# A hybrid DiT backbone on one core: attention queries staged in pairs, turned queries in the unused half of their tile, one square instruction per head

## The chip, the cores and the metric

The kernel runs on one core of a Trainium2 chip. The metric is the device time of one launch in microseconds (us). Three runs of the kernel before gave a median of 2776.6 us (2774.38 to 2782.41).

The core's engines each take their instructions in a fixed order: PE multiplies matrices (PEld is its weight load, which runs beside it), ACT applies functions element by element, DVE combines tensors, POOL does odd jobs and SP issues DMAs. An instruction starts when those ahead of it on its engine have started or ended and when the semaphores it names are reached.

## The reference

A latent stream of 256 tokens (a grid of 4 rows by 64) and a context of 256 tokens, both 2048 wide, go through two layers. Layer 0 mixes tokens by gated-DeltaNet heads (8 of width 128) beside neighbourhood-attention heads (8 of width 128), layer 1 by a short convolution; each has a SwiGLU block of 5632. What matters here is the mixer of layer 0:

```python
def even_mixer(h, hc, w_in, conv_w, a_log, dt_bias, gdn_norm, rpb, w_out, want_ctx):
    pc = hc @ w_in[:, :sum(EVEN_SEGS[:n_seg_c])]            # context: ka va kb vb a b
    ka_c, va_c, kb_c, vb_c, a_c, b_c = segs_c[:6]
    conv_c = short_conv_silu([ka_c, va_c], conv_w)
    k_c = l2norm(heads(conv_c[0]))
    ...
    o_c, s_ctx_fin = gdn_bidirectional(to_bhtd(q_c), to_bhtd(k_c), to_bhtd(v_c), g_c, beta_c, (zeros, zeros))
    ka, va, kb, vb, a, b, qa, qb, za = split_segments(h @ w_in, EVEN_SEGS)
    ka, va, qa = short_conv_silu([ka, va, qa], conv_w)       # conv of 5 taps along the tokens, then silu
    k_l = axial_rope(l2norm(heads(ka)))
    q_l = axial_rope(l2norm(heads(qa))) * HEAD_DIM ** -0.5
    o_l, _ = gdn_bidirectional(to_bhtd(q_l), to_bhtd(k_l), to_bhtd(heads(va)), g_l, beta_l, s_ctx_fin)
    y_gdn = gdn_out_norm(o_l, za, gdn_norm)
    y_na = neighbourhood_attention(heads(qb), heads(kb), heads(vb), k_ctx_na, v_ctx_na, rpb)
    return jnp.concatenate([y_gdn, y_na], axis=-1) @ w_out
```

`l2norm` divides a head's vector by the root of its sum of squares. The gated delta rule works in chunks of 64 tokens and needs the inverse of a triangular matrix for each.

## The kernel before

**Matmuls.** All products are float32 made of three products of rounded parts: each weight tile comes by DMA (`raw`, line 231, 512 KB, 4 buffers), ACT rounds it to `whi` (L174), DVE makes the rest `wlo` (L245), and PE multiplies `whi` by the activations' upper part, `wlo` by it, and `whi` by the lower part. `fm_stream` (matmuls L320) makes features on the partitions, `tm_stream` tokens. Activations of the layer stand in `hA` (first 2 of 16 blocks) and `hB`; `hC` is reloaded later.

**Streams of layer 0, in order.** Keys KA of the gated-delta heads, the gates, queries QA (two streams of four heads, latent tokens only, so 256 wide), values VA (two), and then the attention heads' queries QB (two streams, 256 wide), keys KB and values VB (in turn), the gate ZA, the output projection. Then come layer 0's SwiGLU and layer 1.

**A gated-delta head behind its stream.** `head_evac` makes the evacuation of four heads. `f` copies a head out of PSUM into `hst` (by L169 on ACT or L171 on DVE), and at the fourth head defers a list of steps, one for every step of the next stream: `front` is the convolution of 5 taps (L631 on ACT, four L634 on DVE) and the silu (L636) in a tile `cv` (4 buffers); `back` transposes it to tokens (PE, L193), copies it to `hq` (L174) and, for keys and queries, takes the sums of squares (`hss`, L665). A key head has four tiles of 128 tokens, a query head two, so `back` has four or two squares. `done` follows the fourth `back`. For keys it normalises `hq` (`rstd` with a root at L218 and DVE steps to L222; L681 on ACT; the rotary part L687 to L692 on DVE) and stores it to DRAM as `kd` (L705). For queries it does the same, transposes the result back into a tile `qf`, which is a buffer of the `cv` tag, and stores that as `qTd` (L725). `hq` has the shape [128, 4 token tiles, 4 heads, 128] and 2 buffers (tag `xdT`); a query head set fills 2 of the 4 token tiles.

**The gated-delta chain.** `chunk_matrices` loads the keys by token (`ktok`, L865), turns them (L193 on PE), makes decays (L858, exponential L860) and products (L894, L897), sends the triangles through DRAM (`nd`, `dl`) and solves 32 x 32 blocks in 31 pairs of DVE steps (L938, L940); the solution goes out as `dz` (L947) and comes back as `xd` and `xdT` (L968; `xdT` has the same tag as `hq`). `inverses` combines blocks on PE (L994, L1001, L1007) and `scan` runs the recurrence (L1032 to L1065). It is done for the context first and the latents second.

**Attention queries, keys, values.** `stage` copies a block out of PSUM into a 128 x 512 tile `nst` (3 buffers, tag `nst`), multiplies queries by the scale on the way (L1155, ACT), and stores it (L1156).

**What sets the order.** The program is written as Python generators; `drive` runs a stream and takes one deferred step after each of its steps, `pump` mixes in steps of the modulation (L404 loads, L409 on DVE, L416 on PE), and `plan` calls the inverses at counted steps (P_INV). Behind that a scheduler orders each engine's instructions by a simulated timeline, so a change of one instruction's cost or buffer can move others. On SP, too, a store stands in one row with the weight loads and waits its turn.

Of the kernel before, what the change touches and what calls it, by code (L numbers as in the profile page):

```python
# [23 lines left out]
F32 = mybir.dt.float32  # L24
F32R = mybir.dt.float32r
AF = mybir.ActivationFunctionType
OP = mybir.AluOpType
AX = mybir.AxisListType
# [10 lines left out]
CV = 4  # L39
# [9 lines left out]
R_QB = 0.6  # L49
R_KB = 1.8  # L50
R_ZA = 1.5
R_WO = 2.0
NST = 3
# [10 lines left out]
C_KA, C_VA, C_KB, C_VB, C_AB, C_QA, C_QB, C_ZA = 0, 1024, 2048, 3072, 4096, 4128, 5152, 6176  # L64
# [46 lines left out]
def body(tc, x, c, ctx, c_ctx, ada_w, ada_b, norm_mix, norm_ffn, ffn_w_gate, ffn_w_up, ffn_w_down,  # L111
# [3 lines left out]
    PE, ACT, DVE, POOL, SP = nc.tensor, nc.scalar, nc.vector, nc.gpsimd, nc.sync  # L115
# [43 lines left out]
    def smt():  # L159
        small.append(small.pop(0))  # L160
        return small[0].tile([128, 512], F32, name="sm", tag="sm")
# [3 lines left out]
    def copy(dst, src):  # L165

        flip[0] ^= 1
        if flip[0]:
            ACT.activation(dst, src, AF.Copy)  # L169
        else:  # L170
            DVE.tensor_copy(dst, src)  # L171

    def acopy(dst, src):
        ACT.activation(dst, src, AF.Copy)  # L174
# [16 lines left out]
    def transpose(dst, src):  # L191
        n = src.shape[0]
        return PE.transpose(dst, src, ident[:n, :n])  # L193
# [54 lines left out]
    def w_steps(segs, ks, behind=None):  # L248

        W = sum(s[2] for s in segs)  # L250
        nk = 1024 // W
        for g in range(0, len(ks), nk):
            assert ks[g + nk - 1] == ks[g] + nk - 1
            hi, lo = split_w(load_w(segs, ks[g], nk), behind if g // nk in (2, 3) else None)
            for j in range(nk):
                yield ks[g] + j, hi[:, j * W:(j + 1) * W], lo[:, j * W:(j + 1) * W]
# [3 lines left out]
    def grouped(steps, n, head=1):  # L260


        keep = []
        for i, (k, s) in enumerate(steps):
            keep.append(s)
            if i < head - 1:
                yield i, []
            elif i < n - TAIL:
                yield i, keep[:]
                keep.clear()  # L270
            elif i == n - 1:
                yield i, keep
            else:
                yield i, []
# [33 lines left out]
    def fm_stream(segs, ks, ws, evac, bank=None):  # L308

        nf = sum(s[2] for s in segs) // 128  # L310
        ps = [None] * nf
        for i, group in grouped(((k, (k, hi, lo)) for k, hi, lo in w_steps(segs, ks)), len(ks)):
            for f in range(nf):
                if i == 0:
                    ps[f] = (bank or mmt)()
                for g, (k, hi, lo) in enumerate(group):
                    a, b = hi[:, f * 128:(f + 1) * 128], lo[:, f * 128:(f + 1) * 128]
                    for j, (wt, mv) in enumerate(((a, 0), (a, 1), (b, 0))):
                        o = ps[f][:, 0:len(ws) * 256].rearrange("p (w t) -> p w t", w=len(ws))
                        last_mm[0] = PE.matmul(o, wt, h_(slice(0, len(ws)), mv, k), start=i == 0 and g == 0 and j == 0,  # L320
                                               stop=i == len(ks) - 1 and g == len(group) - 1 and j == 2).ins
                if i == len(ks) - 1:
                    evac(f, ps[f])
            yield
# [56 lines left out]
    def ada_close():  # L381

        for _ in closing[0]:
            yield
# [80 lines left out]
    def defer(f, *args):  # L465

        later.append((f, args))
# [9 lines left out]
    def drive(stream, pump=None, n=1, every=1, counts=False):  # L477
        for i, _ in enumerate(stream):
            steps[0] += counts
            while counts and plan and plan[0][0] <= steps[0]:  # L480
                plan.pop(0)[1]()
            if later and i % every == every - 1:
                f, args = later.pop(0)
                f(*args)
            if pump:
                pump(n)
# [6 lines left out]
    def h_(w, s, k):  # L493
        return hA[:, w, s, k, :] if k < KH else hB[0][:, w, s, k - KH, :]
# [20 lines left out]
    p = smt()  # L515
# [20 lines left out]
    wv = ev_w_in[0]  # L536
    ks = list(range(KT))
# [74 lines left out]
    scale = HD ** -0.5  # L612
# [26 lines left out]
    def head_evac(n, q, c0, done, sums):  # L639

        st_ = {}

        def f(i_, p):
            st_[i_] = kvp.tile([128, 512], F32, name="hst", tag="hst", bufs=6)[:, 0:n * 128]
            copy(st_[i_], p[:, 0:n * 128])
            if i_ < 3:
                return
            out_t = gw.tile([128, 4, 4, 128], F32, name="hq", tag="xdT", bufs=XDT)
            ss = kvp.tile([128, 4, 4], F32, name="hss", tag="hss", bufs=2) if sums else None
            cvs = {}  # L650

            def front(i):
                cvs[i] = conv_silu(st_[i], n // 2, c0 + q * 4 + i)

            def back(i):
                pt = smt()
                for t in range(n):
                    ins = transpose(pt[:, t * 128:(t + 1) * 128], cvs[i][:, t * 128:(t + 1) * 128])
                    if not t:
                        tc.keep_in_program_order(ins)  # L660
                acopy(out_t[:, 0:n, i, :], pt[:, 0:n * 128].rearrange("p (t e) -> p t e", t=n))
                if sums:
                    sq = kvp.tile([128, 128], F32, name="sq", tag="sq", bufs=1)
                    for t in range(n):
                        ACT.activation(sq, out_t[:, t, i, :], AF.Square, accum_out=ss[:, t, i:i + 1])  # L665


            for g_, i in ((front, 0), (front, 1), (front, 2), (back, 0), (front, 3), (back, 1), (None, 0), (back, 2), (back, 3)):
                if g_:
                    defer(g_, i)  # L670
                else:
                    defer(lambda: None)
            defer(done, out_t, ss)
        return f
# [38 lines left out]
    def qa_evac(q):  # L713
        def done(qt, ss):
            rq = rstd(kvp, ss[:, 0:2], [128, 2, 4], 8, 1.0, "rq")
            DVE.tensor_scalar(rq, rq, scale, None, op0=OP.mult)
            normalise(qt, 2, rq)
            for g in range(2):
                qf = kvp.tile([128, 2, 256], F32, name="qf", tag="cv", bufs=CV)
                pt = smt()  # L720
                for i in range(2):
                    for t in range(2):
                        transpose(pt[:, i * 256 + t * 128:i * 256 + (t + 1) * 128], qt[:, t, g * 2 + i, :])
                copy(qf, pt.rearrange("p (i e) -> p i e", i=2))
                SP.dma_start(qTd[:, q * 4 + g * 2:q * 4 + g * 2 + 2, :], qf)  # L725
        return head_evac(2, q, 16, done, True)
# [23 lines left out]
    kvp = pool("kv", stack=kvs, side="right")  # L750
# [7 lines left out]
    pump = Pump([ada_mixer(adap, [(2, "row", None), (3, "sh", None), (4, "sc", g_ffn[0])])], 1, 1)  # L758
# [330 lines left out]
    nsp = pool("stage", stack=lgs, side="right")  # L1089
# [54 lines left out]
    kb_d = dram.tile([128, 8, 512], F32, name="kb_d")  # L1144
    vb_d = dram.tile([128, 4, 1024], F32, name="vb_d")
    qb_d = dram.tile([128, 8, 256], F32, name="qb_d")

    def stage(dst, n, by=None):

        def f(i, *p):  # L1150
            st_ = nsp.tile([128, 512], F32, name="nst", tag="nst", bufs=NST)[:, 0:n]
            if by is None:
                copy(st_, p[-1][:, 0:n])
            else:
                ACT.activation(st_, p[-1][:, 0:n], AF.Copy, scale=by)  # L1155
            SP.dma_start(dst(i), st_)  # L1156
        return f

    for q in range(2):
        drive(fm_stream([(wv, C_QB + q * 512, 512)], ks, [0], stage(lambda f: qb_d[:, q * 4 + f, :], 256, scale)), pump, R_QB, counts=True)  # L1160
    for q in range(2):
        drive(fm_stream([(wv, C_KB + q * 512, 512)], ks, [0, 1], stage(lambda f: kb_d[:, q * 4 + f, :], 512)), pump, R_KB, counts=True)
        drive(tm_stream([(wv, C_VB + q * 512, 512)], ks, lhsh, [0, 1, 2, 3],
                        stage(lambda t: vb_d[:, t, q * 512:(q + 1) * 512], 512)), pump, R_KB, counts=True)
    lga.close()
    yp = pool("y", stack=lgs, side="right")

# [77 lines left out]
    held = na_scores(0)  # L1245
    for h in range(8):
        ahead = na_scores(h + 1) if h < 7 else None
        na_values(h, held)
        held = ahead
# [185 lines left out]
    pump = Pump([ada_job(adp, 1, 2, "row"), ada_job(adp, 1, 4, "sc", gamma=g_ffn[1]), ada_close()], PO, 68)  # L1435
# [7 lines left out]
    for half in range(2):  # L1443
# [17 lines left out]
        for f in range(8):  # L1461
            k = half * 8 + f
            p = smt()
# [5 lines left out]
            cv = dp.tile([128, 256], F32, name="ocv", tag="ocv", bufs=2)  # L1469
# [58 lines left out]
```

## Time and profile before

| | |
|---|---|
| median of three runs | 2776.6 us |
| the profiled execution: time / span | 2776.85 / 2775.1 us |
| granted PE clock, mean | 0.989 |
| instructions | 37687 |
| read from HBM / written | 659.21 / 23.10 MB |
| HBM rate over the span | 246 GB/s |
| PE's largest waits in 160 to 440 us | 6.4 us (ACT cv L636), 6.3 us (ACT nst L1155), 3.0 us (DVE hst L171) |
| squares L665 with their accumulator reads | 48 and 48, from 174.3 to 301.6 us |

The profiled execution took 1.75 us more than its span, which is what lies around it. A share of busy time is a mean over stages with different limits: streams of weights, in which PE never stops, and stages between them in which the chain of the gated-delta heads or the softmax of the attention heads makes it wait. The stages meant in the prediction are stretches of the span in us, and a stage is read by the engine whose busy time fills it and by what PE waits for in it. The chain of waits that ended last reaches back to 713 us only, so the changed place, at 160 to 440 us, is read from windows, waits and the timeline.

### The profile page before, as it was taken

The page shows a single profiled execution, that of the slowest core. Times are in us where ns is not written, and L with a number is a line of the kernel's source. Part 1 is how long each engine was busy: PE and PEld are TensorE (multiplying, and loading weights), DVE is VectorE, ACT ScalarE, POOL GpSimd, SP SyncE. Part 2 cuts the span into 40 slices and gives each one's busy share as a digit, 9 for nine tenths or more (in the row PEclk, how much of TensorE's full clock was granted, in tenths as well). Part 3 has the DMA queues.
Part 4 walks back from the last instruction along what each step waited for, and adds up shares of the span by engine and source line. Part 5 has one row for each costly group of instructions (what it writes and reads, how often), then busy time and mean ns, then how long its engine had stood idle before and what let it go on. Part 6 is the DMA issues. An engine that isn't in the chain of part 4 may idle for free.

```text
span 2775.1 us, 37687 instructions
## 1 busy us (share of the span) xinstructions
PE 2673.2 (96%) x13775; PEld 2192.5 (79%) x13775; DVE 1928.2 (69%) x2653; ACT 1289.3 (46%) x1923; POOL 52.5 (2%) x84
## 2 busy tenths in 40 slices
PE   5999999999989999999999999999999999999998
PEld 2588787887878788888888878788878888888886
DVE  2376786795768888888686667898688644445665
ACT  3267633333554544444455655444454444445554
POOL 0000000101000000000000000000000000000000
PEclk9999999999999999999999999999999999999999
DMA  9954478799748699999785558998669766666553
GB/s 345 325 182 152 146 239 280 233 319 281 231 157 279 227 330 337 347 337 325 276 276 194 193 160 287 328 325 294 199 200 337 239 195 189 187 201 208 195 192 127
DMA packets 287029, 684.81 MB, mean 247 GB/s; under 512 B 57209, under 2 KB 100833, under 8 KB 285307
## 3 DMA queue, kind: packets, MB, share of 16 engines
q1 hardware_dynamic: 280564, 669.26, 71.8%
q10 hardware_dynamic: 4375, 9.48, 1.0%
q0 software_dynamic: 1904, 3.67, 0.4%
q8 instruction: 108, 1.77, 0.2%
q14 instruction: 78, 0.64, 0.1%
HBM read 659.21 MB, written 23.10 MB: 246 GB/s over the span
## 4 chain that ended last, share of the span: by engine, by line
PE 61%; DMA 5%; DVE 4%; issue 3%; ACT 1%; POOLq 0%; POOL 0%; DVEq 0%; SPq 0%; ACTq 0%
PE mm L293 17%; PE mm L296 17%; PE mm L294 17%; DMA araw<-in_ada_w_dram 4%; PE mm L302 2%; PE mm L303 2%; PE mm L304 2%; PE sm L193 1%; DVE acc L374 1%; DVE wlo L245 1%; DMA acc<-in_ada_b_dram 0%; DMA raw<-in_ffn_w_gate_dram 0%; PE sm L1227 0%; PE gd L1074 0%; DVE xc L1301 0%
## 5 line engine op out<-in xcount | busy, mean ns | idle before, releaser
L174 ACT ACTIVATE whi<-raw 128x1024 fp32r<-128x1024 f32 x800 | 843.0, 1060 | 879.5 <-PE mm L296 627.3
L245 DVE TENSOR_TENSOR wlo<-raw,whi 128x1024 fp32r<-128x1024 f32 x800 | 969.7, 1221 | 401.2 <-ACT whi L174 394.4
L294 PE MATMUL mm<-wlo,fhi 128*128 128x512 f32 x1232 | 467.2, 390 | 0.0
L293 PE MATMUL mm<-whi,fhi 128*128 128x512 f32 x1232 | 465.3, 394 | 0.0
L296 PE MATMUL mm<-whi,flo 128*128 128x512 f32 x1232 | 390.5, 390 | 0.1
L374 DVE SCALAR_TENSOR_TENSOR acc<-araw,cT,acc 128x1024 f32<-128x1024 f32 x224 | 287.2, 1282 | 135.8 <-DMA araw<-in_ada_w_dram 125.7
L320 PE MATMUL mm<-hB,whi 128*128 128x512 f32 (+1 forms) x1064 | 278.0, 352 | 1.7 <-DVE hB L580 1.1
L296 PEld LDWEIGHTS mm<-whi,flo 128*128 128x128 f32 x1232 | 230.9, 188 | 49.0 <-DVE flo L1312 0.6
L293 PEld LDWEIGHTS mm<-whi,fhi 128*128 128x128 f32 x1232 | 231.6, 188 | 46.9
L294 PEld LDWEIGHTS mm<-wlo,fhi 128*128 128x128 f32 x1232 | 231.3, 188 | 46.0
L294 PE MATMUL mm<-wlo,ahi 128*128 128x512 f32 x672 | 255.2, 389 | 0.0
L293 PE MATMUL mm<-whi,ahi 128*128 128x512 f32 x672 | 254.4, 390 | 0.0
L320 PEld LDWEIGHTS mm<-hB,whi 128*128 128x128 f32 x1064 | 184.2, 192 | 34.5 <-issue 4.4
L296 PE MATMUL mm<-whi,alo 128*128 128x512 f32 x672 | 207.3, 389 | 0.0
L320 PE MATMUL mm<-hB,wlo 128*128 128x512 f32 (+1 forms) x532 | 180.2, 352 | 0.5 <-DVE wlo L245 0.5
L177 ACT ACTIVATE ahi<-prodT 128x256 fp32r<-128x256 f32 x176 | 73.0, 417 | 188.9 <-PE mm L294 181.9
L409 DVE SCALAR_TENSOR_TENSOR acc<-araw,cT,acc 128x512 f32<-128x512 f32 x192 | 142.5, 746 | 19.7 <-DMA araw<-in_ada_w_dram 16.2
L296 PEld LDWEIGHTS mm<-whi,alo 128*128 128x128 f32 x672 | 126.1, 188 | 26.3
L293 PEld LDWEIGHTS mm<-whi,ahi 128*128 128x128 f32 x672 | 126.2, 188 | 26.0
L294 PEld LDWEIGHTS mm<-wlo,ahi 128*128 128x128 f32 x672 | 126.0, 188 | 26.0
L178 DVE TENSOR_TENSOR alo<-prodT,ahi 128x256 fp32r<-128x256 f32 x176 | 74.3, 424 | 72.8 <-PE mm L296 67.7
L294 PE MATMUL mm<-wlo,dhi 128*128 128x512 f32 x336 | 122.9, 392 | 0.0
(398 smaller groups left out, 3474.7 us busy)
## 6 DMA issues: line engine op xcount, KB each, us to landing
araw<-in_ada_w_dram SPq DMA_DIRECT2D x288, 512.0 KB
raw<-in_ffn_w_down_dram SPq DMA_DIRECT2D x176, 512.0 KB
raw<-in_ffn_w_gate_dram SPq DMA_DIRECT2D x160, 512.0 KB
raw<-in_ffn_w_up_dram SPq DMA_DIRECT2D x160, 512.0 KB
raw<-in_ev_w_in_dram SPq DMA_DIRECT2D x112, 512.0 KB
araw<-in_ada_w_dram SPq DMA_DIRECT2D x192, 256.0 KB
raw<-in_od_w_in_dram SPq DMA_DIRECT2D x96, 512.0 KB
raw<-in_ev_w_out_dram SPq DMA_DIRECT2D x32, 512.0 KB
```

The costliest lines, as they stand in the source:

```text
L174: ACT.activation(dst, src, AF.Copy)
L177: ACT.activation(hi, src, AF.Copy)
L178: (eng or DVE).tensor_tensor(lo, src, hi, op=OP.subtract)
L245: last_lo[0] = DVE.tensor_tensor(lo, raw, hi, op=OP.subtract).ins
L293: PE.matmul(ps[ti][n], a, hi[:, n * 512:(n + 1) * 512], start=first, stop=False)
L294: PE.matmul(ps[ti][n], a, lo[:, n * 512:(n + 1) * 512], start=False, stop=False)
L296: last_mm[0] = PE.matmul(ps[ti][n], b, hi[:, n * 512:(n + 1) * 512], start=False, stop=False).ins
L302: PE.matmul(ps[ti][n], lh(t), hi[:, c_], start=False, stop=False)
L303: PE.matmul(ps[ti][n], lh(t), lo[:, c_], start=False, stop=False)
L320: last_mm[0] = PE.matmul(o, wt, h_(slice(0, len(ws)), mv, k), start=i == 0 and g == 0 and j == 0, stop=i == len(ks) - 1 and g == len(group ...
L374: DVE.scalar_tensor_tensor(acc, raw, cT[:, k:k + 1], acc, op0=OP.mult, op1=OP.add)
L409: DVE.scalar_tensor_tensor(accs[n], raws.pop(i), cT[:, k:k + 1], accs[n], op0=OP.mult, op1=OP.add)
```

## The change

It has three parts.

1. In `back` the squares of a head are one ACT instruction over all its token tiles into a tile of [128, 4, 128] with 2 buffers, and a DVE `tensor_reduce` sums them per token into `hss`. 48 squares with accumulator become 16 squares without and 16 reduces.
2. In `qa_evac` the turned queries are written into token tiles 2 and 3 of their own `hq` tile, in place of a `cv` buffer. A transposed half needs a 128 x 512 place, which one token tile of `hq` is.
3. `stage_pairs` puts two query blocks of 256 in one `nst` tile and stores both with one DMA of 256 KB: four stores in place of eight of 128 KB. `stage` is left with the full-width case.

```diff
@@ -660,9 +660,9 @@
                 acopy(out_t[:, 0:n, i, :], pt[:, 0:n * 128].rearrange("p (t e) -> p t e", t=n))
                 if sums:
-                    sq = kvp.tile([128, 128], F32, name="sq", tag="sq", bufs=1)
-                    for t in range(n):
-                        ACT.activation(sq, out_t[:, t, i, :], AF.Square, accum_out=ss[:, t, i:i + 1])
+                    sq = kvp.tile([128, 4, 128], F32, name="sq", tag="sq", bufs=2)[:, 0:n]
+                    ACT.activation(sq, out_t[:, 0:n, i, :], AF.Square)
+                    DVE.tensor_reduce(ss[:, 0:n, i], sq, axis=AX.X, op=OP.add)
@@ -716,7 +716,7 @@
             for g in range(2):
-                qf = kvp.tile([128, 2, 256], F32, name="qf", tag="cv", bufs=CV)
+                qf = qt[:, 2 + g].rearrange("p h e -> p (h e)").rearrange("p (i e) -> p i e", i=2)
                 pt = smt()
@@ -1145,23 +1145,32 @@
-    def stage(dst, n, by=None):
+    def stage(dst):
...
+    def stage_pairs(dst):
+
+        held = []
+
+        def f(i, p):
+            if not held:
+                held.append(nsp.tile([128, 512], F32, name="nst", tag="nst", bufs=NST).rearrange("p (f t) -> p f t", f=2))
+            ACT.activation(held[0][:, i % 2, :], p[:, 0:256], AF.Copy, scale=scale)
+            if i % 2:
+                SP.dma_start(dst(i - 1), held.pop())
+        return f
+
     for q in range(2):
-        drive(fm_stream([(wv, C_QB + q * 512, 512)], ks, [0], stage(lambda f: qb_d[:, q * 4 + f, :], 256, scale)), pump, R_QB, counts=True)
+        drive(fm_stream([(wv, C_QB + q * 512, 512)], ks, [0], stage_pairs(lambda f: qb_d[:, q * 4 + f:q * 4 + f + 2, :])), pump, R_QB, counts=True)
```

The lines of the changed kernel behind the second part keep their numbers; those behind `stage` are 9 higher.

The order moves. The first place is SP's row of DMAs around the key stores `kd`, before (`-`) and after (`+`): `raw` are weight loads, `ktok` the reloads of the keys, `kTd` and `qTd` stores of turned keys and queries.

```order
-L231 DMA raw<-in_ev_w_in_dram 128x2x512 x7
+L231 DMA raw<-in_ev_w_in_dram 128x2x512 x11
 L705 DMA kd<-hq 512x1x512
-L231 DMA raw<-in_ev_w_in_dram 128x2x512 x2
+L231 DMA raw<-in_ev_w_in_dram 128x2x512
 L865 DMA ktok<-kd 128x2x512
 L231 DMA raw<-in_ev_w_in_dram 128x2x512 x2
 L865 DMA ktok<-kd 128x2x512
 L884 DMA kTd<-kT 128x1024
-L725 DMA qTd<-qf 128x512
-L231 DMA raw<-in_ev_w_in_dram 128x2x512
-L725 DMA qTd<-qf 128x512
+L725 DMA qTd<-hq 128x512 x2
```

The second key store stands behind eleven weight loads since the `kTd` store before it, where it stood behind seven; the reloads of keys that follow it keep their distance to within one load.

The second place is ACT around the scaling of the second key set (`hq<-hq,rkr`), before:

```order
L174 ACTIVATE whi<-raw 128x1024
L665 ACTIVATE sq,hss<-hq 128x128
L681 ACTIVATE hq<-hq,rkr 128x128 x16
L174 ACTIVATE whi<-raw 128x1024
L218 ACTIVATE rqs<-rqv 128x8
L169 ACTIVATE hst<-mm 128x256 x2
L174 ACTIVATE whi<-raw 128x1024
L681 ACTIVATE hq<-hq,rqr 128x128 x8
```

and now:

```order
L636 ACTIVATE cv<-cv 128x256
L169 ACTIVATE hst<-mm 128x256 x2
L174 ACTIVATE whi<-raw 128x1024
L631 ACTIVATE cv<-hst,evcT 128x256
L174 ACTIVATE hq<-sm 128x2x128
L664 ACTIVATE sq<-hq 128x256
L631 ACTIVATE cv<-hst,evcT 128x256 x3
L681 ACTIVATE hq<-hq,rkr 128x128 x16
L218 ACT_TABLE_LOAD
```

The evacuation of the second query stream (`hst<-mm 128x256`) and its first taps (L631) stood behind the sixteen scalings of the keys and now stand ahead of them.

The third place is PE at the second set of inverses (L994, for the latents), which begins, before, inside the last products of a VB stream (`mm` with `hB`; L416 belongs to the modulation):

```order
L293 MATMUL mm<-whi,hB 128x512
L294 MATMUL mm<-wlo,hB 128x512
L296 MATMUL mm<-whi,hB 128x512
L416 MATMUL sm<-cs,acc 128x1 x3
L994 MATMUL gd<-xd,n_4634 32x32
L416 MATMUL sm<-cs,acc 128x1
L994 MATMUL gd<-xd,n_4634 32x32 x31
L302 MATMUL mm<-whi,hB 128x512
```

and now:

```order
L294 MATMUL mm<-wlo,hA 128x512
L296 MATMUL mm<-whi,hA 128x512 x2
L293 MATMUL mm<-whi,hA 128x512
L294 MATMUL mm<-wlo,hA 128x512
L296 MATMUL mm<-whi,hA 128x512
L1060 MATMUL gd<-vd,ktok 128x128 x4
L994 MATMUL gd<-xd,n_4606 32x32 x32
L293 MATMUL mm<-whi,hC 128x512
```

It begins behind the last products with `hA` and directly ahead of the first with the reloaded `hC`, which belong to the stream after. The first set of inverses, for the context, also stands later among the products, by some 20 us of them at their durations in the trace, and behind about 820 us of the profile before PE's order is the same in both.

More of the change, by code (lines that the diff above doesn't have):

```diff
@@ L1146, in body @@
     qb_d = dram.tile([128, 8, 256], F32, name="qb_d")
-    def stage(dst, n, by=None):
+    def stage(dst):
         def f(i, *p):
[L1151 to L1155, printed above, removed]
+            st_ = nsp.tile([128, 512], F32, name="nst", tag="nst", bufs=NST)
+            copy(st_, p[-1])
             SP.dma_start(dst(i), st_)
         return f
+    def stage_pairs(dst):
[7 more added lines that the diff above has]
+        return f
     for q in range(2):
-        drive(fm_stream([(wv, C_QB + q * 512, 512)], ks, [0], stage(lambda f: qb_d[:, q * 4 + f, :], 256, scale)), pump, R_QB, counts=True)
+        drive(fm_stream([(wv, C_QB + q * 512, 512)], ks, [0], stage_pairs(lambda f: qb_d[:, q * 4 + f:q * 4 + f + 2, :])), pump, R_QB, counts=True)
     for q in range(2):
-        drive(fm_stream([(wv, C_KB + q * 512, 512)], ks, [0, 1], stage(lambda f: kb_d[:, q * 4 + f, :], 512)), pump, R_KB, counts=True)
+        drive(fm_stream([(wv, C_KB + q * 512, 512)], ks, [0, 1], stage(lambda f: kb_d[:, q * 4 + f, :])), pump, R_KB, counts=True)
         drive(tm_stream([(wv, C_VB + q * 512, 512)], ks, lhsh, [0, 1, 2, 3],
-                        stage(lambda t: vb_d[:, t, q * 512:(q + 1) * 512], 512)), pump, R_KB, counts=True)
+                        stage(lambda t: vb_d[:, t, q * 512:(q + 1) * 512])), pump, R_KB, counts=True)
     lga.close()
```

## The prediction

> **What bounds the kernel now.** I read the page first (its engine line and its 40 slices), then busy time by stage, then what the matmul engine waits for in the stages that hold the changed lines.
>
> ```profile
> PE 2673.2 (96%) x13775; PEld 2192.5 (79%) x13775; DVE 1928.2 (69%) x2653; ACT 1289.3 (46%) x1923; POOL 52.5 (2%) x84
> ...
> core 0: us, PE busy (x) PEld busy (x) DVE busy (x) ACT busy (x) POOL busy (x), PEclk, DMA share, GB/s
> ...
> 0.00:160.00 160.00, 126.92 (x681) 77.25 (x682) 52.98 (x127) 44.95 (x65) 1.74 (x7) 1.00 0.95 320
> ...
> 219.00:257.00 38.00, 31.07 (x244) 30.18 (x243) 25.57 (x62) 37.47 (x105) 3.26 (x8) 0.94 0.31 90
> 257.00:314.00 57.00, 55.29 (x266) 45.66 (x266) 37.97 (x95) 40.13 (x89) 4.85 (x9) 0.95 0.42 136
> 314.00:367.00 53.00, 50.06 (x234) 41.58 (x235) 44.77 (x87) 22.41 (x31) 2.92 (x3) 0.97 0.61 187
> ...
> 391.00:420.00 29.00, 25.32 (x202) 24.43 (x202) 17.52 (x28) 8.19 (x11) 2.92 (x3) 1.00 0.87 277
> 420.00:440.00 20.00, 17.31 (x247) 13.19 (x247) 10.26 (x15) 6.07 (x12) 0.37 (x1) 0.91 0.88 261
> 440.00:640.00 200.00, 200.00 (x1342) 170.47 (x1341) 169.46 (x322) 63.95 (x116) 14.83 (x27) 1.00 0.84 282
> 640.00:680.00 40.00, 33.96 (x419) 26.35 (x418) 16.26 (x23) 10.78 (x17) 6.59 (x9) 0.83 0.94 260
> ```
>
> PE is busy 96% of the span, so the time falls only where PE has a hole. In 219–257 us it has one of 7 us, and there ACT is busy 37.47 of 38 us: that stage is bound by ACT, an engine with 46% of the span. All the changed lines run in 160–440 us. Behind it, 440–640 us has no hole at all, and its transfers run at 282 GB/s where the first 160 us reached 320, so a stream that starts earlier is fed earlier: what is won ahead of 440 us is carried on, unless 640–680 us takes it.
>
> PE's waits in 160–440 us (in all, times, longest), then their rows on PE's timeline (start, length, in brackets the idle time and who ended it), then the granted clock (behind the busy time) in short stretches:
>
> ```profile
> PE sm L193 <- ACT cv L636: 6.4, 3, 2.8
> PE mm L320 <- ACT nst L1155: 6.3, 4, 2.4
> PE mm L320 <- DVE hst L171: 3.0, 1, 3.0
> ```
> ```profile
> 233.06 0.44 PE L193 MATMUL sm<-cs,cv 128*128 128x128 f32 x2 [0.85 <-ACT cv L636]
> 241.22 0.44 PE L193 MATMUL sm<-cs,cv 128*128 128x128 f32 x2 [2.69 <-ACT cv L636]
> 256.77 1.19 PE L320 MATMUL mm<-hA,whi 128*128 128x512 f32 x2 [3.02 <-DVE hst L171]
> 331.54 1.12 PE L193 MATMUL sm<-cs,cv 128*128 128x128 f32 x4 [2.85 <-ACT cv L636]
> 399.71 0.51 PE L320 MATMUL mm<-hA,whi 128*128 128x256 f32 x2 [1.95 <-ACT nst L1155]
> 432.29 0.72 PE L320 MATMUL mm<-hA,whi 128*128 128x512 f32 x2 [2.45 <-ACT nst L1155]
> ```
> ```profile
> 242.20:245.50 3.30, 3.30 (x18) 0.50 0.32 76
> 255.70:262.60 6.90, 5.83 (x14) 0.51 0.50 175
> 330.85:334.20 3.35, 2.66 (x9) 0.50 0.40 142
> 433.20:436.60 3.40, 3.40 (x10) 0.51 1.04 379
> ```
>
> Three waits make up nearly all of the hole, each with a part of the change against it. And each idle of 2.45 us or more is followed by a stretch at half clock, which costs half of its busy time again: 1.65, 2.9, 1.35 and 1.7 us, together 7.6. The idles of 0.85 and 1.95 us are followed by none. The page "TensorE: Matmul & The Clock Gate" of the Trainium skill (Part 1: The HAM clock gate) puts the drop behind at least one idle window of about 3.4 us. The rows disagree about the length, not the halving.
>
> **The pairs** (stores of attention queries).
>
> ```profile
> ACT nst L1155 <- DMA qb_d<-nst: 15.6, 2, 7.8
> ACT cv L631 <- DMA qTd<-qf: 9.6, 3, 6.5
> ```
>
> ACT waited twice, 15.6 us in all, for a staging buffer whose store was not done, and PE behind it 1.95 and 2.45 us. Eight half-filled buffers become four full ones, with three to hold them: the first six feature blocks need no buffer back, where before only three did. Gain 1.95 + 2.45 + 1.7 of clock = **6.1 us**. Lower bound 2.0: the four KB blocks behind it use the same buffers, and the wait at 432.29 with its clock (4.1) could be handed to one of them. I take 6.1. Its evacuations stay eight, so nothing is added; one DMA of 256 KB replaces two of 128, and SP issues four fewer.
>
> **The queries' tile.** The second row above: ACT's conv tap waited 6.51 us at 328.82 for a `cv` buffer held by a turned-query store; a table load and the silu then run before PE's transposes at 331.54. Without `qf` in that pool the buffer is free. Gain 2.85 + 1.35 = **4.2 us**. The order keeps these stores behind weight loads, so that their tile, one of two, could be given back late to a VA head in the same way: lower bound 0. I take 4.2, and charge half of the 2.85, **1.4**, for a new wait of the silus, since their evacuations now stand in another order.
>
> **The squares.**
>
> ```profile
> L665 ACT ACTIVATE sq<-hq 128x128 f32<-128x128 f32 x48 | 14.6, 304 | 0.7
> L636 ACT ACTIVATE cv<-cv 128x512 f32<-128x512 f32 x16 | 9.7, 621 | 3.7 <-DVE cv L634 3.7
> L636 ACT ACTIVATE cv<-cv 128x256 f32<-128x256 f32 x8 | 3.2, 413 | 0.1
> L636 ACT ACT_TABLE_LOAD x8 | 10.3, 1283 | 0.1
> ```
> ```profile
> 174.28 0.30 ACT L665 ACTIVATE sq<-hq 128x128 f32<-128x128 f32 x1
> ...
> 174.70 0.31 ACT L665 ACTIVATE sq<-hq 128x128 f32<-128x128 f32 x1
> ```
> ```profile
> L1208 DVE TENSOR_REDUCE m<-sm x14: 678/682/692, 680.4 to 807.4; 128x1 f32<-128x512 f32 x14
> ```
>
> A square with its accumulator read takes a place of 0.42 us on ACT (174.28 to 174.70). Eight key heads have four, eight query heads two: 8 × 1.68 + 8 × 0.84 = 20.2 us. One instruction over the whole head is not in the trace; the silus of the same shapes take 0.62 and 0.41 us, so 8 × 0.62 + 8 × 0.41 = 8.2, and ACT gives up **12 us**. In the ACT-bound stage and around it that lifts the idles at 233.06, 241.22 and 256.77 (the hst copy there is late since ACT's and DVE's evacuations take turns): 0.85 + 2.69 + 3.02 + 1.65 + 2.9 = **11.1 us** on PE. Upper bound for more: ACT's 12 us. Lower bound 0, if DVE then holds the same evacuations.
>
> DVE gains 16 reduces. The nearest row reduces 512 elements in 0.68 us; half of that shape I put between 0.34 and 0.68: 8 × 0.68 + 8 × 0.41 = 8.7 us. They lie in stages where DVE is busy 25.57 of 38 and 37.97 of 57 us, so I take 0; without that cover the price is 8.7. The page "VectorE: DVE Perf Modes" of the Trainium skill says to expect the slowest pace of a `tensor_reduce` and to restructure where it is on the hot path, which speaks against this part. Its rule gives no price of its own here.
>
> ACT loads a table whenever its function changes between silu, exponential and root, 1.283 us a load. By the order of the instructions the region to 440 us loses three loads (cover for what is left, taken as 0) and the attention heads behind 680 us gain two in front of their exponentials: up to **2.6 us** back, at least 0 where PE has other work; I take it in full.
>
> **What is late next.** The gated-delta chain: key store, token-wise reload, chunk matrices, solve, inverse.
>
> ```profile
> 217.44 37.57 SPq L231 DMA_DIRECT2D raw<-in_ev_w_in_dram  x7
> ...
> 259.69 0.55 SPq L705 DMA_DIRECT2D kd<-hq  x1
> 260.79 1.73 SPq L231 DMA_DIRECT2D raw<-in_ev_w_in_dram  x2
> ...
> 268.74 4.50 SPq L231 DMA_DIRECT2D raw<-in_ev_w_in_dram  x2
> ```
> ```profile
> L994 PEld LDWEIGHTS gd<-xd,n x384: 101/108/154, 419.2 to 691.1; 32*32 32x32 f32 x128, 64*64 64x64 f32 x64
> ```
>
> SP issues in order, and the second key store is moved behind four more weight loads. The fourth load after 259.69 went out by 273.24, 13.5 us later; less the 11.1 us that PE is ahead by then, the chain is 2.4 us later on the clock. Its first inverse (419.2 us, where PE's weight queue had been held) stands later in PE's order by stream matmuls that take about 19.6 us at their durations in the trace, while PE comes 21.4 us earlier: 1.8 us early. PE would wait there 2.4 + 1.8 = **4.2 us**, between 0 (other steps of the chain have slack) and the 13.5 + 1.8 = 15.3 of no compensation.
>
> **Sum.** −6.1 − 4.2 − 11.1 + 1.4 + 2.6 + 4.2 = −13.2 us from the profiled run's 2776.85, whose span is 2775.1 with 1.75 around it; the median shown is 2776.6, the same for this purpose. Forecast **2764 us**. Moved alone to its worse end, the squares' gain (0) gives 2775, the reduces (8.7) 2772, the chain (15.3) 2775; the new costs all at nothing give 2764 − 4.2 − 2.6 − 1.4 = 2756.
>
> **Rivals.**
>
> *The chain sets the pace.* If the key store slips by the full 13.5 us, PE waits 15.3 at the inverse: −21.4 + 1.4 + 2.6 + 15.3 = −2.1, **2775 us** (2778 with 2.9 of half clock behind it). For it: the weight queue was already held there. Against: the solve's DVE steps lie between stream work, and order leaves 19.6 us more for them.
>
> *Slower, by the SP queue.* In the ACT-bound stage seven loads took 37.57 us, 5.4 each. If the four loads ahead of the key store go at that pace, the store slips 21.5 us, the inverse waits 23.3 and half clock follows it (2.9, as after 256.77), and the pairs keep only 2.0 of their 6.1 because their stores stand in the same queue: −21.4 + 4.1 + 1.4 + 2.6 + 23.3 + 2.9 = +12.9, **2790 us**. With the pairs at 2.0 the other terms come to −13.3, so it decides from 10.4 us of waiting at the first inverse with the clock's 2.9, and can be measured from some 19. Against it: behind 259.69 the loads went at 3.4 us each.
>
> *More is won.*
>
> ```profile
> 646.85 0.21 PE L994 MATMUL gd<-xd,n 32*32 32x32 f32 x2 [1.59 <-DMA xd<-dz]
> 669.54 0.77 PE L293 MATMUL mm<-whi,hC 128*128 128x512 f32 x1 [3.33 <-DMA hC<-h_d]
> ```
>
> 640–680 us has 6.0 us of idle and a clock of 0.83 (0.17 × 33.96 busy = 5.8 us). The second inverse now stands behind the value projection's last matmuls and no longer splits them, so these 11.8 us may go: **2752 us**. For: PE has other work there. Against: the solve that feeds it also stands later.
>
> *The half clock comes by itself.* The slow stretches could fall where they fall, with the 7.6 us staying: 2764 + 7.6 = **2771 us**. By the Trainium skill's window of 3.4 us, on the page named above, these idles would not be the cause. Each of the four stretches begins at such an idle, so I give it little.
>
> *The change frees nothing*: buffers are waited for as before by other tiles. **2777 us**. The order shows the evacuations at other places, which speaks against it.
>
> **How the numbers follow.** A run of this kernel can tell about 0.3% (8.3 us) from no change, so faster means under 2768.3 and slower over 2784.9. Forecast (2757 to 2768) 0.50; more won 0.11; chain 0.18; half clock by itself 0.05; nothing freed 0.05; slower by the queue 0.11. Faster is 0.50 + 0.11 = 0.61, the same 0.28, slower 0.11. The range takes in the chain with its clock, nothing freed, the single ends above and most of the larger gain's own spread: 2748 to 2780, leaving out 0.11 above and about 0.05 below.
>
> **What would show it.** Right: no PE idle over 1 us on nst L1155's successor, no DMA wait of `cv` on the turned queries, ACT clearly below full in the stage of 219–257, 16 squares and 16 reduces, clock 1.00 in those stages, and PE reaching the first hA matmuls of KB about 20 us earlier. The chain is told by a wait at the first L994 rows; the queue by the key store's time. Wrong would be: new half-clock stretches behind waits of silu or of `hq`, DVE full in 219–314 us, or a gain at 440 us that is gone at 680.

## The result and the profile after

The changed kernel took 2769.32 us in the median of ten runs (2762.71 to 2777.47), the kernel before 2776.72; the ratio is 0.9971 with a 95% interval of 0.9957 to 0.9985. One of the ten runs of the kernel before took 8001.77 us; the ratio leaves it out, and without it that median is 2776.6. By the ratio the change is some 8 us faster, surely more than nothing and just under the 0.3% that the prediction called measurable. Forecast were 2764, with a range of 2748 to 2780.

The page of the changed kernel, its engine line, and busy time by the same stages as in the prediction (engines in the same columns, then clock, DMA share and GB/s):

```profile
PE 2668.4 (96%) x13775; PEld 2192.5 (79%) x13775; DVE 1934.8 (70%) x2669; ACT 1280.7 (46%) x1842; POOL 53.7 (2%) x84
```
```profile
219.00:257.00 38.00, 36.12 (x269) 34.79 (x268) 34.02 (x80) 36.66 (x73) 2.78 (x8) 0.96 0.42 124
257.00:314.00 57.00, 57.00 (x289) 48.32 (x288) 41.88 (x97) 37.71 (x72) 4.15 (x9) 1.00 0.42 133
314.00:367.00 53.00, 53.00 (x320) 47.17 (x319) 50.16 (x97) 24.25 (x35) 2.93 (x3) 1.00 0.71 219
...
391.00:420.00 29.00, 29.00 (x164) 24.70 (x162) 17.06 (x22) 8.42 (x11) 1.43 (x2) 1.00 0.89 266
420.00:440.00 20.00, 19.29 (x283) 15.36 (x283) 15.26 (x23) 4.66 (x9) 0.52 (x1) 0.91 0.99 351
440.00:640.00 200.00, 193.33 (x1290) 164.79 (x1288) 160.24 (x310) 64.66 (x116) 20.82 (x33) 0.99 0.84 272
640.00:680.00 40.00, 31.94 (x565) 24.19 (x565) 21.57 (x37) 15.41 (x29) 2.53 (x2) 0.91 0.97 256
680.00:770.00 90.00, 84.53 (x468) 70.01 (x467) 61.46 (x116) 45.72 (x87) 0.00 (x0) 0.94 0.75 242
```

Ahead of 440 us the holes in the changed stages are nearly gone: PE is full in 257–314, 314–367 and 391–420 us and lacks 1.9 us in 219–257. Behind it there are new ones: 440–640 us had none before and has 6.7 us, 640–680 has 8.1 us where 6.0 were, 680–770 has 5.5 where 0.4 were. PE's waits ahead of 440 us and those of 600 to 770 us, after:

```profile
PE sm L193 <- ACT cv L636: 1.9, 1, 1.9
PE mm L320 <- ACT nst L1163: 1.4, 1, 1.4
PE gd L1007 <- issue: 0.7, 1, 0.7
```
```profile
PE gd L994 <- DMA xd<-dz: 9.4, 2, 5.9
PE gd L1052 <- DVE R L1035: 3.2, 1, 3.2
PE mm L293 <- ACT whi L174: 3.0, 2, 2.3
PE mm L293 <- DVE nst L171: 1.5, 1, 1.5
```

and the latter before:

```profile
PE mm L293 <- DMA hC<-h_d: 3.3, 1, 3.3
PE gd L994 <- DMA xd<-dz: 2.7, 3, 1.6
```

To weigh the two sides I cut the span at 440 us and at one instruction, the last product of the attention heads with their values (L1227, L1236 after), which every run but e2 (1.87 us) has with the same wait ahead of it. In before and after (window, its length, PE busy, clock):

```profile
0.00:440.00 440.00, 387.56 (x2441) 0.98 0.71 231
440.00:811.80 371.80, 356.45 (x2602) 0.98 0.78 254
```
```profile
0.00:440.00 440.00, 402.79 (x2569) 0.99 0.76 248
440.00:801.72 361.72, 333.68 (x2474) 0.97 0.77 241
```
```profile
811.80 3.49 PE L1227 MATMUL gd<-PT,vb 128*128 128x256 f32 x8 [3.67 <-ACT PT L169]
```
```profile
801.72 3.78 PE L1236 MATMUL gd<-PT,vb 128*128 128x256 f32 x8 [3.67 <-ACT PT L169]
```

PE's idle time up to 440 us fell from 52.4 to 37.2 us, by 15.2; from there to the mark it rose from 15.3 to 28.0, by 12.7. So only 2.5 us of the idle time won are left at the mark. PE's busy time up to it, for the same 5041 products, fell from 744.0 to 736.5 us, by 7.6. Together the mark comes 10.1 us earlier. What follows the mark is the same work in the same order; it took 1965.0 us of the profiled execution before and 1970.4 after, and between 1965 and 1976 in the other runs below, so a single execution does not show the lead exactly, and the ratio is what counts.

### The profile page after: what moved, and what is told of

It is laid out like the page before. It is cut to its first block, busy times and chain, and to the rows that moved or that the text cites. A ratio compares the mean times of both kernels' runs of the same rounds, so it can differ in the third digit from the quotient of the medians.

```text
span 2770.3 us, 37612 instructions
## 1 busy us (share of the span) xinstructions
PE 2668.4 (96%) x13775; PEld 2192.5 (79%) x13775; DVE 1934.8 (70%) x2669; ACT 1280.7 (46%) x1842; POOL 53.7 (2%) x84
## 5 line engine op out<-in xcount | busy, mean ns | idle before, releaser
L294 PEld LDWEIGHTS mm<-wlo,fhi 128*128 128x128 f32 x1232 | 231.8, 189 | 46.5 <-DVE wlo L245 0.3
```

The source lines that it names most:

```text
L294: PE.matmul(ps[ti][n], a, lo[:, n * 512:(n + 1) * 512], start=False, stop=False)
```

## The experiments

All run the kernel before on the same chip beside them; ratios are to that (over all runs, so they are not the quotients of the medians), and the times expected were set against 2776.7. Three theories came up: the chain (the data of the second inverses come no sooner), the order (the second inverses' new place costs), and, after the first four runs, SP's row (VB's stores behind the reloads).

**e1, the squares alone.**

```diff
-                        ACT.activation(sq, out_t[:, t, i, :], AF.Square, accum_out=ss[:, t, i:i + 1])
+                    ACT.activation(sq, out_t[:, 0:n, i, :], AF.Square)
+                    DVE.tensor_reduce(ss[:, 0:n, i], sq, axis=AX.X, op=OP.add)
```

> The squares alone (one ACT instruction a head, summed by DVE); tile and stores as before. The inverses keep their places of before in PE's order. Chain theory (what is won ahead of 440 us is cut down where PE meets the second set of inverses, whose data come no earlier than the solve and its round trip allow): PE's idles before L994 xd<-dz grow from 2.7 us in all to about 8, and the time is 2771 (between 2768 and 2774). Order theory (the loss comes from the second inverses' new place, right ahead of the first hC product): nothing is given back here, 2766 or less. Both: the idles of 0.85, 2.69 and 3.02 us behind ACT's evacuations go.

2768.1 us, ratio 0.9966 (0.9954 to 0.9978): the squares alone have the whole gain. The waits behind `cv` fell to 3.0 us and that behind `hst` is gone. Idle ahead of L994 was 4.0 us, not 8. Set against 2776.7 the ratio gives 2767.3 us, between the two theories, and the chain theory's sign did not come.

**e2, the tile alone.**

```diff
-                qf = kvp.tile([128, 2, 256], F32, name="qf", tag="cv", bufs=CV)
+                qf = qt[:, 2 + g].rearrange("p h e -> p (h e)").rearrange("p (i e) -> p i e", i=2)
```

> The queries' tile alone (turned queries leave from their own hq tile). Both theories: the 6.51 us that ACT waited for the turned-query store and PE's 2.85 us at 331 go, with the half clock behind them. Chain theory: 2775 (half of 4.2 kept). Order theory: 2773, all kept.

2780.03 us, ratio 1.0004 (0.9992 to 1.0015). The wait at 331 us went, but this order brings a new one ahead of 440 us, in PE's waits there:

```profile
PE mm L320 <- ACT whi L174: 7.4, 1, 7.4
PE mm L320 <- ACT nst L1155: 5.3, 3, 2.9
```

The stores of 128 KB are waited for as before; what keeps the rounding of weights back behind them was not followed up. Both theories had missed it.

**e3, the pairs alone** (the third part of the diff).

> The paired stores alone. The inverses now stand later in PE's order, the second nearly where the whole change has it. Both: PE's waits behind nst L1155 of 1.95 and 2.45 us go. Chain theory: 2773, since the gain ahead of 440 us (6) is smaller than what the chain can follow. Order theory: 2778 or more, because the new place of the second inverses costs more than the pairs win.

2776.32 us, ratio 0.9996 (0.9985 to 1.0007). The waits behind `nst` fell to 1.4 us, as expected, and the second inverses begin at the place of before in PE's order, to within three products, so the order theory did not apply; what came is another wait. PE's and DVE's largest from 600 us:

```profile
PE mm L293 <- DVE nst L171: 11.9, 1, 11.9
```
```profile
DVE nst L171 <- DMA vb_d<-nst: 13.7, 1, 13.7
```

DVE stands 13.7 us at a copy of the values VB, since its staging buffer's store has not gone out, and PE 11.9 us behind it.

**e4, squares and tile.**

> Squares and tile, stores of 128 KB as before; the inverses at their places of before. Chain theory: a bigger gain ahead of 440 us (15) meets the same chain: 2768 to 2771, little better than the squares alone, with some 10 us of idle before L994. Order theory: 2762, the whole of 15 kept.

2767.36 us, ratio 0.9959 (0.9946 to 0.9972): between the two theories, and no worse than the whole change, which has the pairs too. The DVE wait of the changed kernel for VB's store is the longest of its waits from 600 us:

```profile
DVE nst L171 <- DMA vb_d<-nst: 17.2, 1, 17.2
```

and SP's row shows the stores behind the reloads, in the changed kernel:

```profile
639.20 3.19 SPq L968 DMA_DIRECT2D xd<-dz  x2
642.49 0.43 SPq L865 DMA_DIRECT2D vtok<-vd__136  x1
643.02 1.44 SPq L1153 DMA_DIRECT2D vb_d<-nst  x3
```

The stores of three of VB's four blocks went out at 643.02, in one go. DVE had stood at the fourth copy since 634.3 and began it at 651.49. A DVE step that the inverses need (L1009) stands behind it in DVE's row; before, it stands ahead of the copy that waits. But the products whose results that step takes (L1007) ended at 650.78 only, so the copy held the step up by 1.4 us at most, and PE's own wait that names the copy is 1.5 us.

**e5, the whole change with VB's and KB's stores on POOL.**

```diff
-            SP.dma_start(dst(i), st_)
+            POOL.dma_start(dst(i), st_)
```

> The whole change, with the stores of attention keys and values (kb_d, vb_d) issued by POOL in place of SP. PE's order is the same up to the second inverses. SP-row theory (what the pairs win is lost because VB's stores stand in SP's row behind the reloads xd and xdT, so that DVE, at an nst copy, stands 17.2 us and holds back the scan's and the weights' DVE work): that wait falls under 5 us and the time to 2762 (2759 to 2765). Chain theory (the data of the second inverses come no sooner): PE still idles about 9 us before L994 xd<-dz and the time stays at 2767 to 2770.

2765.1 us, ratio 0.9951 (0.9934 to 0.9967); DVE's wait fell to 7.8 us (under 5 was expected), L994's from 9.4 to 4.7, idle behind 440 us from 28.0 to 21.0, and the mark came at 795.57. It is the lowest of all, though its interval meets that of the whole change.

The time is that of the SP-row theory, but the place is not. L994's wait is shorter mainly because PE came to it later: its block of 58 products began at 642.25 us, against 643.15 in the whole change. At the scan's product L1032 at 731 us PE is level with the whole change, and the lead of 6.2 us at the mark arises behind it. In the whole change:

```profile
730.60 1.16 PE L1032 MATMUL gd<-state,kT 128*128 128x128 f32 x8
736.29 2.08 PE L1052 MATMUL gd<-R,xdT 128*128 128x128 f32 x8 [3.20 <-DVE R L1035]
740.64 2.08 PE L293 MATMUL mm<-whi,yhi 128*128 128x512 f32 x4 [2.28 <-ACT whi L174]
748.29 1.06 PE L1032 MATMUL gd<-state,kT 128*128 128x128 f32 x8
```

and here, where PE has no wait between the same two:

```profile
730.86 1.06 PE L1032 MATMUL gd<-state,kT 128*128 128x128 f32 x8
744.53 1.06 PE L1032 MATMUL gd<-state,kT 128*128 128x128 f32 x8
```

Before, these two stand at 746.01 and 756.75 us with 0.3 us of idle between them. The whole change thus led by 15.4 us at the first of them and by 8.5 at the second. `R` is a DVE step of the scan; ahead of it in DVE's row stands the gate's `zst`, for which DVE waited 1.22 us while ACT loaded a table (from 732.58) and then made it. The other wait is for the first weights of the output projection. So neither theory is settled by this run: the data of the second inverses came hardly sooner, and what was won was won elsewhere.

**e6, the whole change with the xdT reloads on ACT.**

```diff
-                SP.dma_start(m_, dz[v, b, q].rearrange(...))
+                (ACT if v else SP).dma_start(m_, dz[v, b, q].rearrange(...))
```

> The whole change, with the xdT half of the reloads of the solve issued by ACT in place of SP. Chain theory: the eight xd loads no longer share a row with eight xdT loads and land some 4 to 6 us sooner, PE's idle before L994 falls from 9.4 to 4 us, and the time to 2764. SP-row theory: VB's stores go out some 5 us sooner, DVE's wait falls from 17 to about 12 us, 2766. If neither counts: 2769.

2773.38 us, ratio 0.9983 (0.9972 to 0.9994), slower than all three theories. The profiled execution took 2781.97 us, 8.6 more than the median, so its waits are larger than the run's usual ones. The reloads did land sooner: the wait for `xd` is gone from PE's list of 600 to 770 us, and DVE's for VB's store fell to 10.9 us. Others took their place:

```profile
PE mm L293 <- DVE nst L171: 8.7, 1, 8.7
PE gd L1052 <- DVE R L1035: 6.9, 1, 6.9
PE gd L994 <- ACT xdT L1011: 4.6, 1, 4.6
PE gd L994 <- issue: 3.4, 1, 3.4
```

**e7, squares and pairs.**

> Squares and pairs, the turned queries in a cv buffer as before. If the tile is worth its 4.2 us beside the others: 2773. If it is worth nothing (as alone): 2769, with the 17 us wait of DVE at VB's nst copy and some 9 us of idle before L994, as in the whole change.

2774.08 us, ratio 0.9987 (0.9976 to 0.9998), with DVE's wait of 15.3 us. Set against the whole change (0.9971) the tile is worth some 4 us beside the other two, though the two intervals meet; alone it was worth nothing.

**e8, squares and tile with VB's and KB's stores on POOL.**

> Squares and tile without the pairs, kb_d and vb_d stores issued by POOL. SP-row theory: DVE's wait at the nst copy of VB (5.2 us in the run of squares and tile) goes, 2763. Chain theory: 2767, as without it.

2767.83 us, ratio 0.9966 (0.9952 to 0.9979): DVE's wait at `nst` is gone, as expected, and nothing is won; PE now idles 7.2 us for `R` (L1035), 6.9 of it at the place where the whole change waits for it.

**e9, the pairs alone with VB's and KB's stores on POOL.**

> The pairs alone, with kb_d and vb_d stores issued by POOL; PE's order is that of the pairs alone up to the second inverses. SP-row theory: PE's 11.9 us behind DVE's nst copy of VB (pairs alone) falls under 4 us and the last L1236 row, at 807.6 there, comes 8 us sooner; 2768. If DVE's wait was only a sign of the chain behind it, PE idles as long elsewhere before 680 us and the time stays at 2776.

2777.86 us, ratio 1.0000 (0.9988 to 1.0013). The wait for DVE's copy is gone, and PE idles as long at the next load, the attention queries' `qb`, which is the second case that was expected:

```profile
PE sm L1212 <- DMA qb<-qb_d: 13.1, 1, 13.1
PE gd L1032 <- DVE state L1065: 5.1, 1, 5.1
```

**e10, the kernel before with VB's and KB's stores on POOL, the control.**

> The kernel before with kb_d and vb_d stores issued by POOL, a control: there DVE waited 2.5 us for a VB store and PE not at all, so SP-row theory gives 2775 (2773 to 2778). If the POOL row helps for another reason (fewer entries in SP's row in general), it gains as in the whole change: 2771 or less.

2785.58 us, ratio 1.0026 (1.0015 to 1.0038): neither case. Idle behind 440 us is 7.5 us more, and 7.2 us of waiting for `R` came at the place where the whole change has it too; the kernel before has 0.3 us of idle there.

**e11, the whole change with both rows moved** (e5 and e6 together).

> The whole change with kb_d and vb_d stores on POOL and the xdT reloads on ACT: both suspects of the second inverses at once. If each of the two rows is a bound of its own: no DVE wait over 4 us at nst, under 3 us of idle before L994, 2758 to 2762. If moving reloads to ACT holds up something else there (as the run with it alone was slower): 2765 or more.

2770.91 us, ratio 0.9971 (0.9960 to 0.9981), as the whole change. PE's wait for `xd` is gone and 9.4 us stand ahead of L994 for `xdT` on ACT, 5.3 for `qb`. Two suspects removed, the same time.

**e12, pairs and tile.**

> Pairs and tile without the squares. The squares carry the gain: 2774 to 2777, with the idles of 3.0 us behind hst and those behind cv at 230 to 260 us still there. If pairs and tile have a worth together that neither has alone: 2770 or less.

2770.53 us, ratio 0.9970 (0.9956 to 0.9984). The idles behind `cv` and `hst` are there (3.6 and 3.0 us), as expected for no squares, and still the kernel is as fast as with them. Two parts that are worth nothing alone are worth the whole gain together.

The whole table, from PE's busy time in the profiled execution of each. Idle is the window less that; "at `R`" is the part of it between the two L1032 rows shown with e5; the mark is the last product named above; tables are ACT's table loads from 680 to 830 us; VB is how SP's row has the second VB stream's four stores:

| parts | idle to 440 | 440 to mark | at `R` | mark | tables | VB stores | ratio |
|---|---|---|---|---|---|---|---|
| before | 52.4 | 15.3 | 0.3 | 811.80 | 7 | 1, 2, 1 | |
| squares | 45.0 | 18.0 | 0.3 | 802.66 | 7 | 1, 2, 1 | 0.9966 |
| tile | 54.8 | 16.5 | 0.0 | 809.08 | 5 | 1, 2, 1 | 1.0004 |
| pairs | 46.5 | 27.6 | 0.0 | 807.59 | 5 | 3, 1 | 0.9996 |
| squares, tile | 41.9 | 17.8 | 0.3 | 799.59 | 7 | 1, 2, 1 | 0.9959 |
| squares, pairs | 40.1 | 28.1 | 6.9 | 809.65 | 9 | 3, 1 | 0.9987 |
| pairs, tile | 44.6 | 17.5 | 0.3 | 800.74 | 7 | 1, 2, 1 | 0.9970 |
| all (after) | 37.2 | 28.0 | 5.5 | 801.72 | 9 | 3, 1 | 0.9971 |
| all, stores on POOL | 38.3 | 21.0 | 0.0 | 795.57 | 7 | (POOL) | 0.9951 |
| all, xdT on ACT | 39.3 | 33.6 | 6.9 | 812.00 | 9 | 3, 1 | 0.9983 |
| all, both | 37.9 | 27.7 | 0.0 | 800.60 | 5 | (POOL) | 0.9971 |
| squares, tile, stores on POOL | 44.2 | 23.0 | 6.9 | 802.73 | 9 | (POOL) | 0.9966 |
| pairs, stores on POOL | 46.9 | 27.6 | 0.0 | 811.78 | 7 | (POOL) | 1.0000 |
| before, stores on POOL | 51.4 | 22.9 | 7.2 | 814.13 | 9 | (POOL) | 1.0026 |

Each line is one execution; that of the pairs alone took 7.6 us more than its run's median, that of e6 8.6. Three things are seen. Up to 440 us every part counts: 7.4 us less idle for the squares, 5.9 for the pairs, 2 to 3 for the tile beside either or both (nothing alone), and 15.2 for all. Behind it, as long as the stores are on SP, the idle time is 15 to 18 us where the scheduler's order lets the first of VB's stores go out alone, and 28 to 34 where three go out in one go behind the reloads. Three of the four kernels with the pairs fell into the second order, pairs and tile into the first. With the stores on POOL the idle time is 21 to 28 us in all five, so VB's stores are not all of it. The third is the column "at `R`": five kernels idle 5.5 to 7.2 us there and all others 0.3 or less, and the five are those with nine table loads behind 680 us. In the same five SP issues seven loads of the output projection's weights in one row that takes 11.8 to 12.8 us. Which of these brings which was not tested.

## Why the prediction was right in direction and too large

*The pairs, 6.1 us; the tile, 4.2; the squares, 11.1.* Their places were right. The idles of 1.95 and 2.45, of 2.85, and of 0.85, 2.69 and 3.02 us are gone after, but for 1.88 us behind `cv` at 244 us, the kind of remainder for which 1.4 was charged, and 1.4 behind `nst`. Of the signs that the prediction named, the 16 squares and 16 reduces came, the wait of `cv` for the turned queries is gone, and KB's first products with `hA` start at 398.90 us, where they started at 420.24. Others did not come: ACT is still busy 36.66 of 38 us in 219–257, the clock there is 0.96, and half clock follows the silu's wait at 244 us, which was a sign of being wrong. As terms of the total they were wrong in kind: worth 9, 0 and 0 us alone in the order squares, tile, pairs, but none of them is worth a fixed sum beside the others.

*The prices of the new instructions.* Both were right. After, on ACT and DVE:

```profile
L664 ACT ACTIVATE sq<-hq 128x512 f32<-128x512 f32 x8 | 4.9, 629 | 0.0
L664 ACT ACTIVATE sq<-hq 128x256 f32<-128x256 f32 x8 | 3.1, 418 | 0.1
```
```profile
L665 DVE TENSOR_REDUCE hss<-sq 128x4 f32<-128x512 f32 x8 | 5.4, 680 | 0.1
L665 DVE TENSOR_REDUCE hss<-sq 128x2 f32<-128x256 f32 x8 | 3.2, 417 | 1.9 <-ACT sq L664 1.8
```

8.0 us on ACT against 8.2 forecast, 8.6 on DVE against 8.7, and no PE wait names the reduces. The prediction set the page "VectorE: DVE Perf Modes" of the Trainium skill (Rules for kernel authors) beside this part, which expects the slowest pace of a `tensor_reduce`. The 0.68 us above is that of a copy of the same size out of PSUM (L171, 683 ns in the trace), and moving the sums there paid: 0.9966 alone.

*The half clock, 7.6 us.* This term was too large. At half clock were 17.1 us up to 440 and 13.7 from there to the mark before, 6.8 and 21.3 after. An estimate of their price, half of PE's busy time in them, gives 7.7 and 6.2 us before, 3.4 and 6.3 after. So ahead of 440 us 4.3 of the 7.6 came: the stretches at 255.7 and 330.9 us went, and those at 242.2 and 433.2 have successors at 244.6 and 428.9. PE's busy time for the same products did fall by 7.6 us, but only 4.2 of it is the clock by this estimate; the rest was not traced, so the agreement is chance. Behind 440 us the new stretches lie in part where PE waits: in one of 10.2 us, 637 to 647, at L994, PE was busy 4.8 us. The rival "the half clock comes by itself" is right in that stretches still come, and wrong for those ahead of 440 us.

*The first inverses, 4.2 us.* This step failed. The key store did go out later in the row, but PE lost only 0.7 us at the first set. What the chain took back, it took at the second set, which the prediction had named only as a place to win: there I read the new place, behind VB's last products, as a gain. The second inverses' own wait grew from 2.7 to 9.4 us. PE reached them 12.1 us sooner than before (633.1 us against 645.3), while the `xd` reloads went out from 630.47 to 642.39, against 639.77 to 650.26, so 9.3 to 7.9 us sooner. With the scan and the weights behind it idle time grew by 12.7 us, where the sum had 4.2 for the chain and 2.6 for table loads.

*The table loads, 2.6 us.* They came as counted: three fewer up to 440 us (19 for 22), two more from 680 us on (9 for 7). Of PE's waits in 600 to 770 us only 0.5 us names the exponentials, but the place at `R`, where these loads stand, has 5.5 us of idle where it had 0.3. So the term may have been too small; that the loads are the cause there is argued from the table, not shown.

*The sum.* Idle: the terms had 13.8 less 1.4 won up to 440 us, and 15.2 came; they had 6.8 given back, and 12.7 came: 8.6 ahead of the L1032 at 731 us, 5.2 behind it at `R`, and 1.1 less in what follows. Clock: 7.6 were forecast, and PE's busy time fell by as much, 4.2 of it by the clock. That makes 10.1 at the mark against 13.2 forecast, and about 8 in the ratio. So the term most at fault is the payback: half of what it was, put at the wrong set of inverses, with the place at `R` counted only in part. That more idle time was won ahead of 440 us, and that the busy time fell beyond the clock, made up for some of it; that is luck.

*What is shown and what is not.* Shown: idle time up to 440 us falls with every part but the tile alone; how much of it is kept is decided behind 440 us, at the second inverses and at `R`; and in the order of the changed kernel VB's stores behind the reloads hold DVE (17.2 us). Not shown: that this wait is what costs the time. Taking the stores out of SP's row cuts the idle time behind 440 us by 7.0 in e5, but PE was level with the whole change until the place at `R`. With squares and tile (e8) the same step won nothing, with the pairs alone (e9) it only moved 12 us of waiting to another load, in the kernel before (e10) it cost 7.5 of idle, nearly all at `R`, and with both rows moved (e11) 9.4 us of waiting came for `xdT`. Open as well is what brings the wait at `R`: no kernel was made that changes only the table loads or only the weight loads there. Transfers are busy 0.91 to 1.05 of the time at 640–680 us in all runs but e2 (0.75); that they bound this stage, so that a wait passes from one load to the next, is argued only. No kernel was made that lowers the bytes or packets of that stage, and no fourth `nst` buffer was tried.

## What to carry to other kernels

A wait that is removed is worth only what the stages behind it let through: here 15.2 us of idle time were won and 12.7 given back. So measure the lead at several fixed instructions behind the change, not the waits that are gone; by the mark alone, e5's gain would seem to come from where the stores stood. In a program whose order a scheduler makes, parts of a change do not add up: two that were worth nothing alone gained 0.3% together; so each combination is timed, not each part. Small ACT instructions with an accumulator read are worth merging where ACT is full: 48 with their reads at 0.42 us became 16 and 16, and this alone gained as much as the whole change (0.9966 and 0.9971).

## What the runs showed of the hardware that had not been expected

The half clock does not need an idle of 2.45 us. After 1.88 us (the row at 244 us) came a stretch at half clock:

```profile
244.12 0.44 PE L193 MATMUL sm<-cs,cv 128*128 128x128 f32 x2 [1.88 <-ACT cv L636]
```
```profile
244.60:248.00 3.40, 3.40 (x18) 0.50 0.11 14
```

In the trace's clock records of both kernels each such stretch inside the span is 3.413 us long, or two or three times that, and all begin at whole multiples of 3.413 us from one another (4, 26, 56, 119 before; 54, 115, 144, 163 after). Cut by that grid from 150 us to the mark, every window at full clock in which PE has 1.88 us or more without an instruction is followed by one at half clock (seven before, four after). None with 0.72 to 1.45 us is; one with 0.71 us is (425.5 to 428.9 us after, among products of 32 x 32). The idle of 1.95 us at 399.71 before, which no half clock followed, lies in two windows, 1.36 us of it in the first. So whether an idle of two microseconds costs clock depends on where it lies on that grid. The page "TensorE: Matmul & The Clock Gate" of the Trainium skill (Part 1: The HAM clock gate) describes a free-running window of this length, and the grid agrees with it; the idle that suffices is shorter here than the whole window that it names.
